# Six operations that wait for transfers keep their program place on their engine

## The chip, the cores and the metric

The kernel runs on one core of a Trainium2 chip. The metric is device time in microseconds (us), the median of three runs. One more execution was recorded by the hardware profiler; its rows are what the text argues from.

## What is computed

One inference step of a small decoder: a pooling layer, then a layer of dilated sliding-window attention, for a prompt of 2048 rows and for 8 single-row samples. Cut to what matters here (the prompt's attention layer):

```
kv = (rmsnorm(h, g_kv) @ w_kv).reshape(B, T, 3, 2, 16, 64)     # keys and values, 3 groups of 16 heads
k  = rope_partial(kv[..., 0, :, :], pos)                       # rotates 16 of the 64 dims of a head
q  = rope_partial((rmsnorm(h, g_b) @ w_in)[q part], pos)
for g, (window, dil) in enumerate(((128, 1), (512, 4), (2048, 16))):
    s = q @ k.T / 8 in blocks of 128, masked to the window;  m = max(s);  p = exp(s - m);  l = sum(p)
    o[g], lse[g] = p @ v / l, m + log(l)
y = sum_g softmax_g(lse) * o[g] * silu(gate);   h = h + y @ w_out;   out = rmsnorm(h, g_final)
```

The kernel also returns the rotated keys and the values of the last rows.

## The kernel before

Products are made to float32 precision from two parts: a value is split into a high part, rounded by a copy (on ACT), and a low part, the difference (on DVE or POOL). A dense product is three matmuls: high by high, low by high, high by low.

After the pooling layer (to about 830 us) and the first half of the rows (to about 1690 us), half 1 works off dense **units** for 8 pairs of heads p, in each for 3 groups g, and in each of these k, q and v: one unit is 48 matmuls of 512 columns on PE into the accumulators `psd` (L241). Beside this dense stream a generator `prompt_attn()` gives the attention, one **step** for each tick of the dense stream: 16 steps for a group, 48 for a pair, 384 in all. A step's scores `pss` (four matmuls, L1211) go through the masked minimum on DVE (L1218), the exponential on ACT (L1224), transposes `ppt` (L1232), their split (`ph` on ACT, L1244; `pl` on DVE, L1248) and the product with the values `ppo` (L1276, L1278). ACT copies half of the product out (`otmp`, L1283) and DVE joins the two halves (`o_add`, L1301).

The operations that the change names stand in these paths:

- A unit's result is copied by ACT into a buffer `raw` (L837), of which three are in use. For k and q, the class `Rope` gathers the rotated rows of two units into `xs` by six DMAs each (`gather`, L782 to L784), multiplies and adds on DVE (`turn`, L790, L791), scatters them back (L794), and some ticks later splits: ACT makes the high part `rh` (L811), it is stored (L812), two ticks later DVE makes the low part in place (L815), and it is stored (L816). The stores of k's output rows (`o_k0` to `o_k2`) read `raw` before that.
- Attention loads k, q and v back (`kt` L1159, `qt` L1161, copied to a second place by POOL, L1163; `vr` L1183, one buffer). `split_v` makes the values' high part on ACT (L1189) and the low part on POOL (L1190).
- After each group, minima and sums are stored and loaded in another layout (`stats_nat`, L1318, L1320, for two of the three groups). `merge` of a pair starts with two minima on DVE (L1329, L1330), and joins the three groups with weights that PE spreads (`pws`, L1359; L1361 on DVE, L1363 on POOL). Joined rows are stored (L1366), and the output phase after the last merge loads them (`cyt`, L1458).

All loads and stores are issued by SP in one queue, in order. `defer(n, f)` runs f n ticks later in program order. The **order on an engine** is not the program's: a scheduler reorders each engine's instructions ahead of time and issues what by its own timing model is ready earliest, so an instruction can stand ahead of ones that were written before it. On the chip each engine then goes through its list in order; an instruction that waits holds all behind it.

Of the kernel before, what the change touches and what calls it, by code (L numbers as in the profile page):

```python
# [12 lines left out]
F32 = mybir.dt.float32  # L13
F32R = mybir.dt.float32r
# [39 lines left out]
def step_kernel(ctx: ExitStack, tc: tile.TileContext, a: dict):  # L54
    nc = tc.nc
    vec, act, pool, pe = nc.vector, nc.scalar, nc.gpsimd, nc.tensor
    load_dma = store_dma = nc.sync.dma_start

    const = ctx.enter_context(tc.tile_pool(name="const", bufs=1))
    dram = ctx.enter_context(tc.tile_pool(name="dram", bufs=1, space=bass.MemoryType.DRAM))  # L60
# [233 lines left out]
    def defer(ticks, fn):  # L294
        deferred.append([ticks, fn])
# [434 lines left out]
    def permd(ap, g):  # L730
        return ap.rearrange("p (r l) -> p r l", r=DIL[g])
# [36 lines left out]
    class Rope:  # L768
# [6 lines left out]
        def gather(self, kind, p, raw):  # L775
            if self.xs is None:
                self.xs = N.bc.tile([P, HALF], F32, name="xs")
            xs, u = self.xs, len(self.units)
            self.units.append((kind, p, raw))
            for b in range(2):  # L780
                x0, r0 = 32 * u + 16 * b, 64 * b
                load_dma(xs[x0:x0 + 16], raw[r0:r0 + 16])  # L782
                load_dma(xs[64 + x0:72 + x0], raw[r0 + 8:r0 + 16])  # L783
                load_dma(xs[72 + x0:80 + x0], raw[r0:r0 + 8])  # L784
            if u == 1:
                defer(3, self.turn)

        def turn(self):
            xs, g = self.xs, self.g
            vec.tensor_tensor(permd(xs, g), permd(xs, g), perm(N.cs2, g), OP.mult)  # L790
            vec.tensor_add(xs[0:64], xs[0:64], xs[64:128])  # L791
            for u, (kind, p, raw) in enumerate(self.units):
                for b in range(2):
                    load_dma(raw[64 * b:64 * b + 16], xs[32 * u + 16 * b:32 * u + 16 * b + 16])  # L794
                defer(3 + 2 * u, lambda kind=kind, p=p, raw=raw: self.split(kind, p, raw))

        def dst(self, kind, p, x):
            v = qkd[kind][self.g][p].rearrange("h d x n -> (h d) x n")[:, x]
# [2 lines left out]
        def split(self, kind, p, raw):  # L801
            g = self.g
            if kind == 1:
                if g == 2:
                    store_dma(a["o_k2"][self.hf, p], raw)
                elif self.hf == 1 and g == 0:
                    store_dma(a["o_k0"][p], raw[:, HALF - P:])
                elif self.hf == 1:
                    store_dma(a["o_k1"][p], permd(raw, g)[:, :, P:])
            rh = N.bw.tile([P, HALF], F32R, name="rh", bufs=1)  # L810
            act.activation(rh, raw, AF.Copy)  # L811
            store_dma(self.dst(kind, p, 0), permd(rh.bitcast(F32), g))  # L812

            def low():
                vec.tensor_sub(raw.bitcast(F32R), raw, rh.bitcast(F32))  # L815
                store_dma(self.dst(kind, p, 1), permd(raw, g))  # L816
                if self.hf == 1:
                    done[p, g] = done.get((p, g), 0) + 1
            defer(2, low)
# [312 lines left out]
    def prompt_attn():  # L1132
# [52 lines left out]
        def split_v(ci):  # L1185
            b0 = first_block(ci)
            vr = V[ci][:, b0:].rearrange("p b (h d) -> p b h d", h=2)
            vt = V[ci] = tl.tile([P, 5, 2, 2, 64], F32R, name="vt")
            act.activation(vt[:, b0:, :, 0], vr, AF.Copy)  # L1189
            pool.tensor_sub(vt[:, b0:, :, 1], vr, vt[:, b0:, :, 0].bitcast(F32))  # L1190

        def prevs(g, c):
# [93 lines left out]
        def o_add(i):  # L1286
            ci, h = i // 4, (i // 2) % 2
            p, g, c = where(ci)
            r0 = 64 * h
            if g == 0 and h == 0:  # L1290
                OT[p, 0, c] = tot.tile([P, 512], F32, name="ot0", bufs=5)
            elif c == 0 and h == 0:
                OT[p, g] = tot.tile([P, SEQ], F32, name=f"ot{g}")
            ot = (OT[p, 0, c] if g == 0 else OT[p, g])[r0:r0 + 64]
            if g == 2:
                act.activation(ot.rearrange("p (l r) -> p r l", r=16)[:, 4 * c:4 * c + 4],
                               PO.pop(i // 2)[0:64].rearrange("p (r l) -> p r l", r=4), AF.Copy)
                return
            po, otmp = PO.pop(i // 2)
            dst = ot if g == 0 else ot.rearrange("p (l r) -> p r l", r=4)[:, c]  # L1300
            vec.tensor_add(dst, po[0:64], otmp)  # L1301

        def stats_nat(p, g):

# [19 lines left out]
        def merge(p):  # L1324


            cst = CST.pop(p)
            mm = tst.tile([P, 2, 16], F32, name="mm")
            vec.tensor_tensor(mm, cst[:, 0, 0:2], cst[:, 1, 0:2], OP.min)  # L1329
            vec.tensor_tensor(mm, mm, cst[:, 2, 0:2], OP.min)  # L1330
            ee = tst.tile([P, 3, 2, 16], F32, name="ee")
            vec.tensor_sub(ee, mm[:, None].to_broadcast([P, 3, 2, 16]), cst[:, :, 0:2])
            act.activation(ee, ee, AF.Exp)
            el = tst.tile([P, 3, 2, 16], F32, name="el")
            vec.tensor_tensor(el, ee, cst[:, :, 2:4], OP.mult)
            vec.tensor_add(mm, el[:, 0], el[:, 1])
            vec.tensor_add(mm, mm, el[:, 2])
            vec.reciprocal(mm, mm)
            vec.tensor_tensor(ee, ee, mm[:, None].to_broadcast([P, 3, 2, 16]), OP.mult)
            yield  # L1340
            ws = tst.tile([P, 6, 2, 16], F32R, name="ws")
            e6 = ee.rearrange("p g h x -> p (g h) x")
            act.activation(ws[:, :, 0], e6, AF.Copy)
            vec.tensor_sub(ws[:, :, 1], e6, ws[:, :, 0].bitcast(F32))
            store_dma(wrow[p].rearrange("r (t x) -> t r x", x=16),
                      ws.bitcast(F32).rearrange("p r i x -> p (r i) x"))
            yield
            yield
            load = lambda e: load_dma(spread[e % 2][0:12], wrow[p][:, 512 * e:512 * e + 512])
            load(0)  # L1350
            load(1)
            for _ in range(4):
                yield
            for e in range(4):
                cs_ = slice(512 * e, 512 * e + 512)
                out = OT[p, 0, e]
                for g in range(3):
                    ps = ps_tile("s", "pws")
                    pe.matmul(ps, sel[:, g], spread[e % 2].bitcast(F32R), start=True, stop=True)  # L1359
                    t_ = OT[p, g][:, cs_] if g else out  # L1360
                    vec.tensor_tensor(t_, ps, t_, OP.mult)  # L1361
                    if g:
                        pool.tensor_add(out, out, t_)  # L1363
                    yield
                d0 = cs_.start + (NB if cs_.start >= HALF else 0)
                defer(2, lambda out=out, d0=d0: store_dma(yd[p][:, d0:d0 + 512], out))  # L1366
                if e < 2:
                    load(e + 2)
# [251 lines left out]
```

## Time and profile before

| what | us |
|---|---|
| median of 3 runs | 3481.15 (3475.03 to 3481.45) |
| the profiled execution | 3495.7 |
| its span | 3493.7 |
| PE busy in the span | 3212.7 |
| half 1 with attention, 1820 to 3200: PE busy of 1380 | 1296.6 |
| the same: DVE, ACT, POOL busy | 837.5, 941.7, 541.8 |

Busy time counts matmuls by a modelled end. The granted clock is the share of TensorE's full 2.4 GHz that the chip gave it in a stretch; 0.5 is 1.2 GHz. A wait in the profile is idle time of an engine just before an instruction, named with what ended it.

### The profile page before, as it was taken

What the parts mean: (1) busy time and instruction counts of PE and PEld (TensorE: products, weight loads), DVE (VectorE), ACT (ScalarE), POOL (GpSimd) and SP (SyncE); (2) the same over time, 40 slices, a digit from 0 to 9 for tenths busy, and PEclk for the clock granted to TensorE, in tenths of its full rate; (3) what the DMA queues carried; (4) which work ended last, traced back from release to release, by engine and by line L of the source; (5) the groups of instructions that cost most, each with busy time, mean ns of one, the idle gap of its engine ahead of it and who ended that gap; (6) DMA issues with size and microseconds to landing.
All of it is one profiled execution on the core that took longest, in us unless ns stands there. A gap on an engine that the chain in (4) does not pass through costs nothing.

```text
span 3493.7 us, 56933 instructions
## 1 busy us (share of the span) xinstructions
PE 3212.7 (92%) x19608; PEld 2821.1 (81%) x19608; DVE 2086.5 (60%) x4061; ACT 1715.9 (49%) x3812; POOL 1516.5 (43%) x954
## 2 busy tenths in 40 slices
PE   8999999899998898987999999899999999999798
PEld 8887778789888887886778788788778878887698
DVE  6745665526766677677346565656565756564445
ACT  3343433324434343343236667675667666778221
POOL 5666765633334354343333343434343434342342
PEclk9999999999999999998999999999999999999899
DMA  4435452424576766767776767676676777775554
GB/s 134 149 123 167 133 165 98 133 91 133 157 196 194 184 196 184 191 203 198 198 219 172 193 183 191 185 172 183 170 202 175 192 182 190 202 193 137 188 154 121
DMA packets 547742, 596.94 MB, mean 171 GB/s; under 512 B 216904, under 2 KB 407752, under 8 KB 547448
## 3 DMA queue, kind: packets, MB, share of 16 engines
q1 hardware_dynamic: 547456, 593.32, 60.7%
q8 instruction: 156, 2.56, 0.3%
q14 instruction: 130, 1.06, 0.1%
HBM read 371.77 MB, written 184.04 MB: 159 GB/s over the span
## 4 chain that ended last, share of the span: by engine, by line
PE 30%; DMA 11%; DVE 6%; SPq 4%; ACT 4%; issue 3%; POOL 1%; DVEq 0%; ACTq 0%; POOLq 0%
PE psd L241 19%; PE pss L1211 3%; PE ppt L1232 3%; DMA statd<-st 1%; PE ppo L1276 1%; DMA xs<-raw 1%; DMA o_k<-raw 1%; PE ppo L1278 1%; ACT pr L1224 1%; DVE xs L791 1%; DMA spb<-pd 1%; PE ppo L1273 1%; DMA raw<-xs 1%; SPq L783 1%; DMA vr<-vd 1%
## 5 line engine op out<-in xcount | busy, mean ns | idle before, releaser
L1163 POOL CAST qt<-qt 64x1024 fp32r<-64x1024 f32 x192 | 209.5, 1091 | 549.4 <-DMA qt<-qd 480.2
L1224 ACT ACTIVATE pr<-pr,st 128x256 f32<-128x256 f32 (+1 forms) x768 | 345.7, 452 | 168.1 <-DVE st L1218 166.3
L1218 DVE CUSTOM_DVE_ANT_0 pr<-pss,mask 128x256 f32<-128x256 f32 (+1 forms) x768 | 248.9, 359 | 154.8 <-PE pss L1211 86.4
L1248 DVE TENSOR_TENSOR pl<-ppt,ph 128x512 fp32r<-128x512 f32 (+2 forms) x384 | 216.9, 569 | 134.1 <-ACT ph L1244 132.0
L168 POOL TENSOR_TENSOR ringl<-wst,ringh 128x1024 fp32r<-128x1024 f32 x96 | 241.3, 2516 | 126.6 <-ACT ringh L163 74.9
L1211 PE MATMUL pss<-kt,qt 128*128 128x256 f32 (+1 forms) x1536 | 268.9, 292 | 27.6 <-DVE st L1218 16.5
L1211 PEld LDWEIGHTS pss<-kt,qt 128*128 128x128 f32 x1536 | 229.0, 199 | 47.2 <-DVE st L1218 18.9
L241 PE MATMUL psd<-hn_2h,ringh 128*128 128x512 f32 x640 | 260.6, 407 | 4.2 <-ACT raw L837 2.4
L241 PE MATMUL psd<-hn_2l,ringh 128*128 128x512 f32 x640 | 259.7, 406 | 5.1 <-DVE hn_2l L644 5.1
L163 ACT ACTIVATE ringh<-wst 128x1024 fp32r<-128x1024 f32 x184 | 193.4, 1052 | 142.2 <-PE psd L241 94.5
L241 PE MATMUL psd<-hn_3h,ringh 128*128 128x512 f32 x640 | 259.6, 406 | 3.0 <-ACT raw L837 1.5
L127 POOL TENSOR_TENSOR wst<-wst,gvec 128x1024 f32<-128x1024 f32 x88 | 178.7, 2033 | 192.1 <-DMA wst<-in_wKV 117.0
L241 PE MATMUL psd<-hn_3l,ringh 128*128 128x512 f32 x640 | 258.8, 404 | 2.2 <-DVE hn_3l L644 2.2
L241 PE MATMUL psd<-hn_2h,ringl 128*128 128x512 f32 x640 | 259.8, 406 | 0.0
L241 PE MATMUL psd<-hn_3h,ringl 128*128 128x512 f32 x640 | 259.3, 405 | 0.0
L1244 ACT ACTIVATE ph<-ppt 128x512 fp32r<-128x512 f32 (+2 forms) x384 | 190.7, 501 | 114.2 <-PE ppt L1232 111.4
L1232 PE MATMUL ppt<-ident,pr 128*128 128x128 f32 x1200 | 211.2, 284 | 22.0 <-DVE pl L1248 10.1
L168 DVE TENSOR_TENSOR ringl<-wst,ringh 128x512 fp32r<-128x512 f32 x176 | 141.6, 841 | 123.3 <-ACT ringh L163 122.9
L1276 PE MATMUL ppo<-ph,vt 128*128 128x128 f32 (+1 forms) x688 | 175.2, 282 | 27.5 <-DVE ot L1301 10.3
L970 PE MATMUL pwx<-t1h,ringh 128*128 128x256 f32 (+1 forms) x576 | 172.1, 299 | 30.3 <-DVE pairl L924 15.8
L1190 POOL TENSOR_TENSOR vt<-vr,vt 128x512 fp32r<-128x512 f32 (+1 forms) x96 | 142.5, 1484 | 127.7 <-ACT vt L1189 107.7
L1232 PEld LDWEIGHTS ppt<-ident,pr 128*128 128x128 f32 x1200 | 145.4, 144 | 49.1 <-issue 11.8
(298 smaller groups left out, 9769.6 us busy)
## 6 DMA issues: line engine op xcount, KB each, us to landing
qt<-qd SPq DMA_DIRECT2D x192, 256.0 KB
wst<-in_wKV SPq DMA_DIRECT2D x72, 512.0 KB
kt<-kd SPq DMA_DIRECT2D x288, 128.0 KB
wst<-in_wA SPq DMA_DIRECT2D x64, 512.0 KB
wst<-in_wQ SPq DMA_DIRECT2D x52, 512.0 KB
kd<-rh SPq DMA_DIRECT2D x48, 512.0 KB
qd<-rh SPq DMA_DIRECT2D x48, 512.0 KB
vd<-vt SPq DMA_DIRECT2D x96, 256.0 KB
```

What stands on the lines that cost most here:

```text
L127: pool.tensor_tensor(st, st, gs[:, :, None].to_broadcast([P, KT, P]), OP.mult)
L163: act.activation(self.w[0], self.st, AF.Copy)
L168: self.eng.tensor_sub(self.w[1][:, k], self.st[:, k], self.w[0][:, k].bitcast(F32))
L241: pe.matmul(ps[:, :n], u[:, k, ws], v[:, k, c0:c1], start=(k, i) == order[0], stop=(k, i) == order[-1])
L1163: pool.tensor_copy(qr[64:128], qr[0:64])
L1211: pe.matmul(ps[:, sl], qt[:, x, qc], kt_[:, kc], start=x == 0, stop=x == 1)
L1218: vec.tensor_tensor_reduce(pr[:, lo:], ps[:, sl], mask[:, lo:], 1.0, BIG, OP.add, OP.min, st[:, 0, h, col:col + 1])
L1224: act.activation(pr[:, lo:], pr[:, lo:], AF.Exp, bias=st[:, 0, h, col:col + 1], scale=-1.0, accum_out=st[:, 1, h, col:col + 1])
L1232: pe.transpose(pt[:, (2 * bb + x) * P:(2 * bb + x + 1) * P], pr[:, x * P:(x + 1) * P], ident)
L1244: act.activation(PB[i][0][:, s], pv[:, s], AF.Copy)
L1248: vec.tensor_sub(PB[i][1][:, s], pv[:, s], PB[i][0][:, s].bitcast(F32))
L1276: pe.matmul(po[:, q0:q1], vt[:, kb + 1, h].rearrange("p x d -> p (x d)"), xh, start=first, stop=False, skip_group_check=True)
```

## The change

`tc.keep_in_program_order(ins)`, called `pin` here, ties an instruction to the one written just before it on the same engine: the scheduler may not put it ahead of that one. It adds no wait on the chip. Pinned are L790, L811, L815, L1189, L1301 and L1329. Two counts of ticks change with it: `turn` is deferred by 4 - hf and the split by 4 - hf + 2u, so that half 1 (hf = 1) keeps 3 and 3 + 2u, and half 0 waits a tick longer. Lines of the changed kernel are two higher from L58 on.

```
@@ -55,6 +55,8 @@
     nc = tc.nc
     vec, act, pool, pe = nc.vector, nc.scalar, nc.gpsimd, nc.tensor
     load_dma = store_dma = nc.sync.dma_start
+
+    pin = tc.keep_in_program_order
 
     const = ctx.enter_context(tc.tile_pool(name="const", bufs=1))
     dram = ctx.enter_context(tc.tile_pool(name="dram", bufs=1, space=bass.MemoryType.DRAM))
@@ -783,16 +785,16 @@
                 load_dma(xs[64 + x0:72 + x0], raw[r0 + 8:r0 + 16])
                 load_dma(xs[72 + x0:80 + x0], raw[r0:r0 + 8])
             if u == 1:
-                defer(3, self.turn)
+                defer(4 - self.hf, self.turn)
 
         def turn(self):
             xs, g = self.xs, self.g
-            vec.tensor_tensor(permd(xs, g), permd(xs, g), perm(N.cs2, g), OP.mult)
+            pin(vec.tensor_tensor(permd(xs, g), permd(xs, g), perm(N.cs2, g), OP.mult))
             vec.tensor_add(xs[0:64], xs[0:64], xs[64:128])
             for u, (kind, p, raw) in enumerate(self.units):
                 for b in range(2):
                     load_dma(raw[64 * b:64 * b + 16], xs[32 * u + 16 * b:32 * u + 16 * b + 16])
-                defer(3 + 2 * u, lambda kind=kind, p=p, raw=raw: self.split(kind, p, raw))
+                defer(4 - self.hf + 2 * u, lambda kind=kind, p=p, raw=raw: self.split(kind, p, raw))
 
         def dst(self, kind, p, x):
             v = qkd[kind][self.g][p].rearrange("h d x n -> (h d) x n")[:, x]
@@ -808,11 +810,11 @@
                 elif self.hf == 1:
                     store_dma(a["o_k1"][p], permd(raw, g)[:, :, P:])
             rh = N.bw.tile([P, HALF], F32R, name="rh", bufs=1)
-            act.activation(rh, raw, AF.Copy)
+            pin(act.activation(rh, raw, AF.Copy))
             store_dma(self.dst(kind, p, 0), permd(rh.bitcast(F32), g))
 
             def low():
-                vec.tensor_sub(raw.bitcast(F32R), raw, rh.bitcast(F32))
+                pin(vec.tensor_sub(raw.bitcast(F32R), raw, rh.bitcast(F32)))
                 store_dma(self.dst(kind, p, 1), permd(raw, g))
                 if self.hf == 1:
                     done[p, g] = done.get((p, g), 0) + 1
@@ -1186,7 +1188,7 @@
             b0 = first_block(ci)
             vr = V[ci][:, b0:].rearrange("p b (h d) -> p b h d", h=2)
             vt = V[ci] = tl.tile([P, 5, 2, 2, 64], F32R, name="vt")
-            act.activation(vt[:, b0:, :, 0], vr, AF.Copy)
+            pin(act.activation(vt[:, b0:, :, 0], vr, AF.Copy))
             pool.tensor_sub(vt[:, b0:, :, 1], vr, vt[:, b0:, :, 0].bitcast(F32))
 
         def prevs(g, c):
@@ -1298,7 +1300,7 @@
                 return
             po, otmp = PO.pop(i // 2)
             dst = ot if g == 0 else ot.rearrange("p (l r) -> p r l", r=4)[:, c]
-            vec.tensor_add(dst, po[0:64], otmp)
+            pin(vec.tensor_add(dst, po[0:64], otmp))
 
         def stats_nat(p, g):
 
@@ -1326,7 +1328,7 @@
 
             cst = CST.pop(p)
             mm = tst.tile([P, 2, 16], F32, name="mm")
-            vec.tensor_tensor(mm, cst[:, 0, 0:2], cst[:, 1, 0:2], OP.min)
+            pin(vec.tensor_tensor(mm, cst[:, 0, 0:2], cst[:, 1, 0:2], OP.min))
             vec.tensor_tensor(mm, mm, cst[:, 2, 0:2], OP.min)
             ee = tst.tile([P, 3, 2, 16], F32, name="ee")
             vec.tensor_sub(ee, mm[:, None].to_broadcast([P, 3, 2, 16]), cst[:, :, 0:2])
```

Every operation and every transfer is the same in both programs, but for two more table loads on ACT (38 against 36). Up to about 1690 us of the trace and from about 3255 us on, all engines have the same order. In between it differs; counted in attention steps, L790, L815 and L811 move back by 16 to 17 steps on average, L1329 by 14, L1189 by 0.4, L1301 by about 0.

DVE at the merge of the sixth pair, before (`pr`, `st` are the scores' minima, `mm` the merge's):

```order
L1248 TENSOR_TENSOR pl<-ppt,ph 128x384
L1301 TENSOR_TENSOR ot_27312<-ppo,otmp 64x512
L1248 TENSOR_TENSOR pl<-ppt,ph 128x512
L1329 TENSOR_TENSOR mm<-cst 128x32
L1218 ISA pr,st_27750<-pss,mask 128x128
L1218 ISA st_27750 128x1
```

and in the changed program:

```order
L1220 ISA pr,st_27750<-pss,mask 128x128
L1220 ISA st_27750 128x1
L1250 TENSOR_TENSOR pl<-ppt,ph 128x2x128
L1324 COPY cst<-st_27750 128x64
L1331 TENSOR_TENSOR mm<-cst 128x32
L1332 TENSOR_TENSOR mm<-mm,cst 128x32
L1334 TENSOR_TENSOR ee<-mm,cst 128x96
```

L1329 (L1331 in the changed program) stood among the minima of the pair's last group; now it stands behind the copy L1322 that ends the pair's statistics, and the second minimum follows at once.

DVE at the low part of one raw buffer, raw_25205, before (with the numbers of the tiles):

```order
L1218 ISA pr_24863,st1_24838<-pss_24839,mask_15543 128x128
L1218 ISA st1_24838 128x1
L1218 ISA pr_24865,st1_24838<-pss_24839,mask_15543 128x256
L1218 ISA st1_24838 128x1
L815 TENSOR_TENSOR raw_25205<-raw_25205,rh_25948 128x1024
L1361 TENSOR_TENSOR ot2_23700<-pws_24867,ot2_23700 128x512
L168 TENSOR_TENSOR ringl_181<-wst_25778,ringh_180 128x512 x2
```

and in the changed program:

```order
L1220 ISA pr_25976,st2_25571<-pss_25956,mask_15543 128x128
L1220 ISA st2_25571 128x1
L1220 ISA pr_25978,st2_25571<-pss_25956,mask_15543 128x128
L1220 ISA st2_25571 128x1
L1250 TENSOR_TENSOR pl_25923<-ppt_25919,ph_25922 128x2x128
L817 TENSOR_TENSOR raw_25205<-raw_25205,rh_25948 128x1024
L1250 TENSOR_TENSOR pl_25967<-ppt_25963,ph_25966 128x2x128
L1220 ISA pr_26029,st2_25571<-pss_26007,mask_15543 128x128
```

The low part stood 140 rows further ahead, just behind the minima of the step that reads pss_24839; now it stands among steps with pss_25956 and pss_26007.

PE from the middle of step 260 on (a row with x4 is four matmuls), before:

```order
L241 MATMUL psd<-hn_3h,ringh 128x512
L1211 MATMUL pss<-kt,qt 128x128 x2
L1211 MATMUL pss<-kt,qt 128x256 x6
L1232 MATMUL ppt<-ident,pr 128x128 x4
L1276 MATMUL ppo<-ph,vt 128x256
L1278 MATMUL ppo<-pl,vt 64x256
L1276 MATMUL ppo<-ph,vt 128x128
L1278 MATMUL ppo<-pl,vt 64x128
L241 MATMUL psd<-hn_3l,ringh 128x512
L241 MATMUL psd<-hn_3h,ringl 128x512
```

and in the changed program:

```order
L243 MATMUL psd<-hn_3h,ringl 128x512
L1213 MATMUL pss<-kt,qt 128x128 x2
L1213 MATMUL pss<-kt,qt 128x256 x2
L1234 MATMUL ppt<-ident,pr 128x128 x2
L1213 MATMUL pss<-kt,qt 128x256 x4
L1278 MATMUL ppo<-ph,vt 128x256
L1280 MATMUL ppo<-pl,vt 64x256
L1278 MATMUL ppo<-ph,vt 128x128
L1280 MATMUL ppo<-pl,vt 64x128
L1234 MATMUL ppt<-ident,pr 128x128 x2
L1213 MATMUL pss<-kt,qt 128x128 x2
```

Before, psd matmuls of the dense units come back after one step. In the changed program the next one stands just ahead of the scores of step 272 (steps are counted from 0). Counted over all 384 steps: runs of at least four steps without a psd matmul are five with 29 steps before, and eight with 69 steps now. Ahead of the first scores of the groups that start at steps 224, 256, 272, 304, 320, 352 and 368, blocks of 55, 31, 65, 47, 82, 54 and 110 psd matmuls stand without attention; before, no block was longer than 26.

## Rows read from the trace of the kernel before

**Rows 1.** The page, busy time of the engines: us, share of the span, instructions.

```profile
PE 3212.7 (92%) x19608; PEld 2821.1 (81%) x19608; DVE 2086.5 (60%) x4061; ACT 1715.9 (49%) x3812; POOL 1516.5 (43%) x954
```

**Rows 2.** Busy time by stage: stretch, its length, busy us (instructions) of PE, PEld, DVE, ACT and POOL, the granted clock of PE, the DMA share, GB/s.

```profile
1690.00:1820.00 130.00, 119.06 (x517) 95.20 (x516) 52.89 (x69) 37.83 (x56) 45.28 (x23) 0.96 0.73 204
1820.00:3200.00 1380.00, 1296.60 (x8044) 1120.37 (x8043) 837.45 (x2364) 941.72 (x2453) 541.79 (x399) 0.96 0.71 186
3200.00:3323.00 123.00, 98.39 (x563) 85.54 (x562) 50.21 (x120) 55.03 (x111) 37.54 (x37) 0.86 0.51 160
```

**Rows 3.** Who waited for whom, 1820 to 3200 us: engine, tile and line <- what ended the wait: us in all, times, longest.

```profile
DVE mm L1329 <- DMA cst<-statd: 43.5, 7, 9.9
ACT vt L1189 <- DMA vr<-vd: 39.7, 14, 7.8
DVE raw L815 <- DMA o_k<-raw: 38.9, 15, 5.5
...
DVE ot L1301 <- DMA yd<-ot: 28.6, 12, 4.0
...
DVE xs L790 <- DMA xs<-raw: 20.5, 13, 3.5
ACT rh L811 <- DMA raw<-xs: 19.5, 15, 3.3
...
ACT rh L811 <- DVE raw L815: 7.4, 6, 2.3
```

**Rows 4.** The timeline of DVE, then of PE, around 2820 us: start, us, operation, and in brackets the idle time ahead of it and what ended it.

```profile
2825.88 0.19 DVE L1329 TENSOR_TENSOR mm<-cst 128x32 f32<-128x32 f32 x1 [9.89 <-DMA cst<-statd]
...
2826.54 0.69 PE L1211 MATMUL pss<-kt,qt 128*128 128x128 f32 x2 [5.62 <-DVE st L1218]
```

**Rows 5.** Busy time ahead of that gap and with it, columns as in Rows 2.

```profile
2812.00:2820.00 8.00, 8.00 (x52) 7.07 (x51) 3.00 (x9) 3.97 (x12) 1.03 (x1) 1.00 0.72 78
2820.00:2830.00 10.00, 4.38 (x18) 3.46 (x17) 3.22 (x12) 4.67 (x13) 1.26 (x1) 0.69 0.45 111
```

**Rows 6.** Busy time in the five stretches without a psd matmul, columns as in Rows 2; then, of L241 alone, the sum over the five; then, of L1211 alone (PE, PEld, clock, DMA), the first and the last of the five, which have 107 matmuls in all.

```profile
2052.00:2068.00 16.00, 11.72 (x54) 9.80 (x53) 11.25 (x27) 10.26 (x26) 7.61 (x5) 0.62 0.87 249
2243.60:2270.50 26.90, 18.60 (x106) 17.45 (x107) 19.10 (x57) 20.56 (x56) 11.55 (x9) 0.75 0.76 224
2458.00:2470.00 12.00, 8.30 (x48) 7.66 (x48) 9.71 (x23) 9.17 (x25) 1.25 (x2) 0.72 0.93 189
2588.90:2604.00 15.10, 8.85 (x44) 7.52 (x43) 11.45 (x27) 8.58 (x20) 5.37 (x6) 0.71 0.76 230
2788.00:2801.00 13.00, 8.61 (x50) 7.51 (x49) 10.31 (x25) 10.19 (x30) 5.28 (x5) 0.74 0.85 259
...
sum 83.00, PE 0.00 PEld 0.05; mean PE 0.00 PEld 0.01
...
2052.00:2068.00 16.00, 4.75 (x19) 3.79 (x17) 0.62 0.87 249
...
2788.00:2801.00 13.00, 4.13 (x20) 3.31 (x19) 0.74 0.85 259
```

**Rows 7.** Who waited in these stretches: the first and the last of the four long waits of PE (3.8, 3.1, 3.8 and 4.0 us).

```profile
PE pvt L861 <- DVE pl L1248: 3.8, 1, 3.8
...
PE ppo L1276 <- ACT rh L811: 4.0, 1, 4.0
```

**Rows 8.** Groups of instructions by line, ACT in 1690 to 3323 us: count | busy us, mean ns of one | idle ahead of them and what ended it.

```profile
L1224 ACT ACTIVATE pr<-pr,st 128x256 f32<-128x256 f32 (+1 forms) x768 | 345.7, 452 | 168.1 <-DVE st L1218 166.3
...
L1244 ACT ACTIVATE ph<-ppt 128x512 fp32r<-128x512 f32 (+2 forms) x384 | 190.7, 501 | 114.2 <-PE ppt L1232 111.4 <-DVE st L1218 0.5
...
L1283 ACT ACTIVATE otmp<-ppo 64x512 f32<-64x512 f32 x128 | 76.3, 596 | 36.2 <-DVE ot L1301 33.4
```

**Rows 9.** Of L837 alone, one of the lines that tell what it waited for: us, times.

```profile
  DMA kd<-raw: 2.3, 1
```

**Rows 10.** The chain that ended last, in order of time (start, us, what): a low or high part stored, a q load. Then the group of POOL's copy of q, and two psd matmuls in PE's timeline.

```profile
2335.70 5.78 DMA kd<-rh
...
1797.06 5.40 DMA qt<-qd
...
L1163 POOL CAST qt<-qt 64x1024 fp32r<-64x1024 f32 x192 | 209.5, 1091 | 549.4 <-DMA qt<-qd 480.2
...
2813.01 0.40 PE L241 MATMUL psd<-hn_3h,ringh 128*128 128x512 f32 x1
2813.24 0.39 PE L241 MATMUL psd<-hn_3l,ringh 128*128 128x512 f32 x1
```

**Rows 11.** The tail: busy time of L241 alone in the last merge; PE's timeline at the first pws of that merge and at the first matmul of the output phase; the group of L1361.

```profile
3227.00:3255.00 28.00, 23.91 (x94) 17.11 (x93) 1.00 0.19 63
...
3230.70 0.74 PE L1359 MATMUL pws<-spread,sel 128*128 128x512 f32 x2 [0.95 <-DMA spread<-wrow]
...
3267.04 0.58 PE L241 MATMUL psd<-cy0h,wbh 128*128 128x288 f32 x1 [12.52 <-DMA cyt<-yd]
...
L1361 DVE TENSOR_TENSOR ot<-pws,ot 128x512 f32<-128x512 f32 x96 | 65.5, 684 | 25.6 <-PE pws L1359 21.7 <-ACT ot L1296 3.5
```

**Rows 12.** Groups of instructions by line, table loads of ACT.

```profile
L1224 ACT ACT_TABLE_LOAD x10 | 12.8, 1283 | 0.2
```

More of the change, by code (lines that the diff above doesn't have):

```diff
@@ L57, in step_kernel @@
     load_dma = store_dma = nc.sync.dma_start
+    pin = tc.keep_in_program_order
     const = ctx.enter_context(tc.tile_pool(name="const", bufs=1))
@@ L785, in gather @@
             if u == 1:
-                defer(3, self.turn)
+                defer(4 - self.hf, self.turn)
         def turn(self):
             xs, g = self.xs, self.g
-            vec.tensor_tensor(permd(xs, g), permd(xs, g), perm(N.cs2, g), OP.mult)
+            pin(vec.tensor_tensor(permd(xs, g), permd(xs, g), perm(N.cs2, g), OP.mult))
             vec.tensor_add(xs[0:64], xs[0:64], xs[64:128])
@@ L794, in turn @@
                     load_dma(raw[64 * b:64 * b + 16], xs[32 * u + 16 * b:32 * u + 16 * b + 16])
-                defer(3 + 2 * u, lambda kind=kind, p=p, raw=raw: self.split(kind, p, raw))
+                defer(4 - self.hf + 2 * u, lambda kind=kind, p=p, raw=raw: self.split(kind, p, raw))
         def dst(self, kind, p, x):
@@ L810, in split @@
             rh = N.bw.tile([P, HALF], F32R, name="rh", bufs=1)
-            act.activation(rh, raw, AF.Copy)
+            pin(act.activation(rh, raw, AF.Copy))
             store_dma(self.dst(kind, p, 0), permd(rh.bitcast(F32), g))
             def low():
-                vec.tensor_sub(raw.bitcast(F32R), raw, rh.bitcast(F32))
+                pin(vec.tensor_sub(raw.bitcast(F32R), raw, rh.bitcast(F32)))
                 store_dma(self.dst(kind, p, 1), permd(raw, g))
@@ L1188, in split_v @@
             vt = V[ci] = tl.tile([P, 5, 2, 2, 64], F32R, name="vt")
-            act.activation(vt[:, b0:, :, 0], vr, AF.Copy)
+            pin(act.activation(vt[:, b0:, :, 0], vr, AF.Copy))
             pool.tensor_sub(vt[:, b0:, :, 1], vr, vt[:, b0:, :, 0].bitcast(F32))
@@ L1300, in o_add @@
             dst = ot if g == 0 else ot.rearrange("p (l r) -> p r l", r=4)[:, c]
-            vec.tensor_add(dst, po[0:64], otmp)
+            pin(vec.tensor_add(dst, po[0:64], otmp))
         def stats_nat(p, g):
@@ L1328, in merge @@
             mm = tst.tile([P, 2, 16], F32, name="mm")
-            vec.tensor_tensor(mm, cst[:, 0, 0:2], cst[:, 1, 0:2], OP.min)
+            pin(vec.tensor_tensor(mm, cst[:, 0, 0:2], cst[:, 1, 0:2], OP.min))
             vec.tensor_tensor(mm, mm, cst[:, 2, 0:2], OP.min)
```

## The prediction

> **What bounds the kernel now.** I read the page first: PE is busy 92% of the span [rows 1], so the time is PE's work plus what PE loses by waiting and by a low clock. Then the busy time by stage [rows 2]. The change moves instructions only between 1690 us and the merge of the last pair at about 3255 us (the order is the same, instruction for instruction, before and after that), so the stage to look at is half 1 with its attention, 1820 to 3200 us. There PE is busy for 1296.6 of 1380 us at a mean granted clock of 0.96: PE's work at the full clock is about 1296.6 x 0.96 = 1245 us, and the loss is 135 us, 83 us of it idle and 52 us clock. No other engine comes near (ACT 942, DVE 837, DMA share 0.71). What can be won here is at most these 135 us, and what can be lost has no such bound.
>
> Third, who waited for whom in that stage [rows 3]. These of its rows belong to the change: on DVE the merge's first minimum L1329 (43.5 us), the low part L815 (38.9), the rotation L790 (20.5); on ACT the high part L811 (19.5, and 7.4 for L815); then the values' high part L1189 (39.7) and the joining L1301 (28.6). Each is an instruction that stands at the head of an in-order engine while its transfer flies, with attention's own operations behind it. One case shows the whole mechanism [rows 4]: L1329 holds DVE for 9.89 us, L1218 stands behind it, and PE, whose next scores wait for a buffer that L1218 frees, has a gap of 5.62 us. The granted clock was 1.00 in the 8 us before; over the 10 us with the gap it was 0.69, partly at 1.2 instead of 2.4 GHz [rows 5]. So a wait costs its gap and some clock behind it.
>
> Fourth, where dense matmuls (psd of the units) are missing beside attention. Five stretches of 83 us in all have no psd matmul, and there PE is busy only 56.1 us, at clocks of 0.62 to 0.75 [rows 6]. Busy time by clock gives 39.9 us of work, so 43 us are lost: a third of the stage's loss in 6% of its time. The scores' matmuls count 107 in them, four to a step, so 27 steps: 1.49 us of work and 1.6 us of loss for each.
>
> **The change part by part.** Nothing is computed otherwise. By the order, measured in attention steps, L790, L815 and L811 move back by 16 to 17 on average, L1329 by 14. L1329 then stands right behind L1322, 14 steps (of 1380/384 = 3.6 us, an estimate: about 50 us) later than before; L790 stands 4 to 17 steps behind its gather where it was about 1, and the six DMAs of the gather have 2 to 5 us to land. So I take these waits as gone. L1301 and L1189 move by less than half a step on average: their waits stay, pins or not. Moved are 43.5 + 38.9 + 20.5 + 19.5 + 7.4 = 130 us of wait, not moved 39.7 + 28.6 = 68 [rows 3], a share of 0.655.
>
> Term 1, the waits outside the psd-free stretches: the loss there is 135 - 43 = 92 us. Taken in proportion to the waits, 0.655 x 92 = 60 us go and 32 stay. This is an estimate; its ends are 92 (all PE loss follows these waits) and about 30 (what is freed meets the next wait in half of the cases).
>
> Term 2, the psd-free stretches. The pins tie the release of a raw buffer (L815, then its store L816) to attention's progress, and the dense stream, which in before ran some 75 to 130 matmuls ahead of attention, can no longer do so. By the order, before has five runs of four or more steps without a psd matmul, 29 steps; after has eight, 69 steps. The price of one step decides the sum. As measured it is 1.6 us, but 14.7 of the 26.9 us that PE idled in these stretches are four gaps that stand right behind a wait of L815 or L811 [rows 7], which go. 12.2 us of idle stay, and of the 16.3 us of clock I keep half: 20.4 us over 27 steps, 0.8 us a step. Its lower end is the pace of ACT, which has the most to do in a step: (345.7 + 190.7 + 76.3)/384 = 1.6 us [rows 8] against PE's 1.49, 0.1 us a step. The upper end is 1.6, if the pinned waits were not what made these stretches slow. With 0.8 the stretches lose 69 x 0.8 = 55 us where they lost 43.
>
> The Trainium skill, page "Perfetto Trace Analysis", section Optimization Strategy, speaks against the change here: where a kernel has regimes that are limited by different engines, it advises to interleave them, and the new order interleaves less. By that rule the step keeps the price that the stretches have now, 1.6 us; the rival below has the time. The rows of the five stretches agree with it.
>
> Term 3, raw buffers. After the change L815 comes on average 4.7 steps ahead of the first write (L837) of the same buffer's next user, where it was 13.7; in 16 of 42 cases it is at most 2. L837 then can wait for the store on ACT, with attention's exponentials behind it. Before shows one such wait, of 2.3 us [rows 9]. At 0 to 1.5 us of PE time for each of the 16 that is 0 to 24; I take 8, since a part is already in term 2.
>
> Term 4, starts of groups. From step 224 on, attention has caught up with the dense stream at seven group starts: on PE 31 to 110 psd matmuls stand in one block ahead of the group's first scores, while SP's queue has only some five DMAs, or none, between the last store of the group's q and its first load. The chain store, load, cast is 5.78 + 5.40 + 1.09 = 12.3 us [rows 10]. A psd matmul takes 0.233 us, start to start [rows 10], so the blocks cover 7.2 us (31), 10.9 (47) and 12.6 us or more (54 to 110): uncovered are 5 and 1.4, together 6 us. The ends are 0 and 7 x 12.3 = 86.
>
> Term 5, the tail. In before, 23.9 us of psd matmuls run between 3227 and 3255 us beside the last merge [rows 11]; in after they are done earlier and the 12 pws stand together. From 3227 us before takes 40.0 us to the first matmul of the output phase (3267.04). After needs 3.7 us to the first pws (3230.70), 12 x 0.684 = 8.2 for L1361, about 1 for the last and the 12.5 us that the first output matmul waits for its load: 25.4, and 23.9 us of psd earlier, +9 us. The ends are -3 (its loads issued during the merge) and +15.
>
> The rest costs nothing that I can find: two table loads more on ACT, 1.28 us each [rows 12], beside PE work on an engine with a third of its time free (if not hidden, 2.6 us). In half 0 the pins and the shifted ticks change no instruction's place.
>
> **Sum.** Stage loss 135 becomes 32 + 55 + 8 + 6 = 101, so -34; the tail adds 9: -25 us. The profiled execution took 3495.7 us, which makes 3470.7; the median of the runs lies 14.5 us under the profiled one, and carries the same change: 3481.15 - 25 = 3456 us.
>
> **Rivals.** (a) Slower: the psd-free steps keep the price of today. 69 x 1.6 = 110 instead of 55 us: the sum is +30 us, 3511. For it: each of the five stretches of before has a low clock, and a clock that is low makes PE itself the slow link there (2243.6 to 2270.5: 18.6 us busy at 0.75). Against it: the four gaps behind pinned waits. It decides from 25/69 us above my value, at about 1.16 us a step.
>
> The Trainium skill, page "TensorE: Matmul & The Clock Gate", section Why this matters for your kernels, warns of idle gaps between bursts of matmuls because the clock falls back to half. The trace agrees where PE had its 5.62 us gap; whether the clock holds in a long attention-only run without such gaps no row here shows.
>
> (b) Slower: group starts uncovered. If the last stores are later than the order makes them look (L816 waits for L815, which is now behind attention steps), all seven chains stand open: +80 us on my sum, 3536. It decides when stores are issued after the dense block begins to run out.
>
> (c) The gain is larger: the stretches run at ACT's pace, 0.1 us a step, 7 us in all: -73, 3408.
>
> (d) No net change: price near 1.16, or what goes at L1329 and L815 returns at L1301, L1189 and L837: about 3481. That the pins do nothing is excluded for four of the six lines by the order; for L1301 and L1189 it is what I expect.
>
> **How the numbers follow.** About 7 us (0.2%) is what a measurement of this kernel can tell from no change. Forecast 0.51, (c) 0.11: faster 0.62. (d) 0.16: same. (a) 0.16, (b) 0.06: slower 0.22. The range must reach (c) and most of (a): 3408 to 3505 leaves out (b), the far end of (a) and what lies beyond (c), in all about 0.18.
>
> **What would show it.** L1329, L790, L815 and L811 should nearly vanish from the list of waits, with L1189 and L1301 at 40 and 30 us or more. PE's busy time times clock in 1820 to 3200 us should stay near 1245 us. The psd-free stretches should be longer, some 69 steps, and their loss by step reads off term 2 directly: 0.8 for me, 1.6 for (a), 0.1 for (c). L837 shows term 3, PE's gaps ahead of pss at seven group starts term 4, the stretch between the last L1322 and the first output matmul term 5. I am wrong if the waits stay where they are, or if the clock in attention-only runs is as low without gaps as with them.

## The result, and the profile after

The changed kernel takes 3526.33 us (3521.99 to 3539.61, 4 runs) beside 3481.3 us of before: 1.0136 of it, 95% interval 1.0120 to 1.0152. It is slower, by about 47 us, and outside the range. The profiled execution of after has a span of 3523.2 us, that of before 3493.7; so the two traces differ by 29.5 us, less than the medians (45): the profiled execution of before is 14 us above its median, that of after close to its own. The accounts below are of these two executions.

Half 1 with attention first, the stretch of [rows 2], from the busy time by stage (columns as there):

```profile
1820.00:3200.00 1380.00, 1286.74 (x7916) 1109.33 (x7915) 830.36 (x2319) 921.82 (x2396) 538.79 (x390) 0.96 0.69 182
```

PE is busy for 10 us less than before at the same clock, and does 128 matmuls less in the same time. To see where the time goes, I cut the work from 1690 us to the end into three pieces, for every kernel in the same way: up to the last scores (the last pss), from there to the first matmul of the output phase, and the rest. The loss of a piece is its length less PE's busy time by the granted clock, summed over slices of 5 us. Of the first piece the stretches without psd matmuls are taken by themselves (between two psd matmuls with at least 14 pss between them).

| us | before | changed |
|---|---|---|
| loss up to the last pss | 138.7 | 153.5 |
| of it in stretches without psd | 46.9 (34 steps) | 69.8 (77 steps) |
| of it outside them | 91.7 | 83.8 |
| loss from the last pss to the output phase | 13.7 | 27.6 |
| output phase | 226.6 | 223.3 |

23 us come from the stretches and 14 from the last merge; the waits outside give back 8 and the output phase 3. These are 25.5 us. Both pages count the same 19608 matmuls (that of before in [rows 1], this that of the changed kernel):

```profile
PE 3219.5 (91%) x19608; PEld 2819.0 (80%) x19608; DVE 2084.1 (59%) x4061; ACT 1719.5 (49%) x3814; POOL 1521.1 (43%) x954
```

Up to 1690 us the order of the two is the same; but the 9400th matmul starts at 1702.9 us before and at 1697.6 in the changed kernel, so from there on the changed execution is 35 us longer. Some 9 us of these the pieces do not explain, and that stays open.

Who waited, 1820 to 3200 us, columns as in [rows 3] (lines are two higher):

```profile
ACT vt L1191 <- DMA vr<-vd: 70.1, 20, 11.9
...
DVE ot L1303 <- DMA yd<-ot: 42.4, 19, 5.9
...
ACT raw L839 <- DMA kd<-raw: 22.1, 9, 7.0
...
ACT rh L813 <- DMA raw<-xs: 20.2, 11, 3.6
...
DVE ot L1303 <- ACT otmp L1285: 19.6, 14, 12.4
...
DVE raw L817 <- DMA o_k<-raw: 12.8, 5, 7.1
...
PE psd L243 <- ACT raw L839: 11.2, 7, 3.8
...
DVE raw L817 <- DMA kd<-rh: 7.2, 1, 7.2
DVE raw L817 <- issue: 6.2, 1, 6.2
```

The merge's minimum (43.5 us before) and the rotation (20.5) have no row any more. The low part's wait for the output rows fell from 38.9 to 12.8, with 13.4 us of two waits at the same line that before did not have. The high part still waits for its transfer as it did (19.5 before). And three waits for transfers grew: the values' high part from 39.7 to 70.1, the joining from 28.6 to 42.4, and L839 (L837 of before), which hardly waited for a store before [rows 9], now waits 22.1 us for raw buffers to be stored, with PE's psd matmuls behind it. What went is 43.5 + 20.5 + 26.1 + 7.4 = 97.5 us, what came is 30.4 + 13.8 + 22.1 + 13.4 = 80.

This list leaves out other waits at the same lines: the joining's wait for `otmp`, above all, fell from 34.7 to 19.6 us. All idle time ahead of the six pinned lines and L837, whatever ended it, was 276 us before and is 233 now. So 43 us of wait did go on DVE and ACT, and PE's loss outside the stretches fell by 8.

The stretches without psd matmuls, as in [rows 6], with the sum of L243 alone and the first and the last row of L1213 alone (308 pss in all, 77 steps):

```profile
1837.60:1864.60 27.00, 21.95 (x161) 20.40 (x160) 24.06 (x65) 23.61 (x61) 11.28 (x9) 0.87 0.78 216
2045.00:2071.40 26.40, 20.18 (x141) 17.47 (x139) 24.62 (x64) 22.74 (x62) 11.92 (x9) 0.94 0.80 225
2372.70:2387.50 14.80, 10.98 (x61) 9.57 (x60) 11.23 (x29) 9.95 (x29) 5.08 (x4) 0.77 0.80 186
2563.40:2596.10 32.70, 23.78 (x167) 20.40 (x165) 28.29 (x75) 27.05 (x76) 14.31 (x10) 0.95 0.78 211
2766.10:2797.30 31.20, 22.94 (x164) 20.62 (x163) 26.96 (x71) 27.19 (x76) 12.28 (x9) 0.89 0.77 191
2849.30:2860.20 10.90, 8.71 (x70) 8.03 (x69) 6.44 (x26) 10.83 (x31) 2.32 (x2) 0.84 0.83 254
2964.20:2993.80 29.60, 21.34 (x133) 19.02 (x131) 25.48 (x55) 23.16 (x61) 8.93 (x5) 0.81 0.69 156
3036.10:3062.10 26.00, 20.10 (x151) 18.56 (x150) 17.17 (x65) 22.91 (x66) 9.81 (x8) 0.79 0.83 238
...
sum 198.60, PE 3.24 PEld 0.58; mean PE 0.41 PEld 0.07
...
1837.60:1864.60 27.00, 8.15 (x44) 6.66 (x44) 0.87 0.78 216
...
3036.10:3062.10 26.00, 8.51 (x44) 7.83 (x44) 0.79 0.83 238
```

There are eight stretches instead of five, at clocks of 0.77 to 0.95 instead of 0.62 to 0.75. A step costs 69.8/77 = 0.91 us there; it cost 1.4 before by the same cut. ACT and DVE are busy for 84% and 83% of these stretches.

The tail: DVE's copy that ends the last statistics, PE's first pws of the last merge and its first output matmul, then the busy time of that stretch:

```profile
3262.27 0.20 DVE L1324 COPY cst<-st 128x64 f32<-128x64 f32 x1 [1.60 <-ACT pr L1226]
...
3272.10 0.73 PE L1361 MATMUL pws<-spread,sel 128*128 128x512 f32 x2 [3.38 <-DMA spread<-wrow]
...
3299.84 0.58 PE L243 MATMUL psd<-cy0h,wbh 128*128 128x288 f32 x1 [16.99 <-DMA cgt<-sgd]
...
3267.10:3299.80 32.70, 8.99 (x25) 4.04 (x23) 13.37 (x24) 8.12 (x13) 14.20 (x13) 0.59 0.71 206
```

PE is busy for 9 of 32.7 us, at a clock of 0.59; before, 23.9 us of psd matmuls stood in the merge [rows 11].

A start of a group, at step 224 (2600 us): SP's store of q's low part, its load of the group's q, POOL's copy of it and PE's first scores:

```profile
2597.68 0.39 SPq L818 DMA_DIRECT2D qd<-raw  x1
...
2608.78 1.83 SPq L1163 DMA_DIRECT2D qt<-qd  x3
...
2617.22 1.03 POOL L1165 CAST qt<-qt 64x1024 fp32r<-64x1024 f32 x1 [12.37 <-DMA qt<-qd]
...
2618.31 1.97 PE L1213 MATMUL pss<-kt,qt 128*128 128x128 f32 x8 [3.45 <-POOL qt L1165]
```

From the store's issue to the first scores 20.6 us go by, and not the 12.3 of the forecast: SP issues the load 11.1 us behind the store, and in between the rest of a gather, another gather, and attention's loads of k and v. The block of 55 psd matmuls covers all but 3.45 us of it. Slice by slice the seven starts lose some 12 to 14 us together, by where a slice is cut from the stretches beside it.

### The profile page after: what moved, and what is told of

Same layout as the page of the kernel before. It is cut to its first block, busy times and chain, and to the rows that moved or that the text cites. A ratio compares the mean times of both kernels' runs of the same rounds, so it can differ in the third digit from the quotient of the medians.

```text
span 3523.2 us, 56875 instructions
## 1 busy us (share of the span) xinstructions
PE 3219.5 (91%) x19608; PEld 2819.0 (80%) x19608; DVE 2084.1 (59%) x4061; ACT 1719.5 (49%) x3814; POOL 1521.1 (43%) x954
## 4 chain that ended last, share of the span: by engine, by line
PE 33%; DMA 9%; DVE 6%; SPq 4%; ACT 3%; issue 3%; POOL 1%; DVEq 0%; ACTq 0%; POOLq 0%
PE psd L243 21%; PE pss L1213 3%; PE ppt L1234 2%; PE pwx L972 1%; DMA wst<-in_wKV 1%; DMA cyt<-yd 1%; PE ppo L1278 1%; DVE pr L1220 1%; PE ppo L1275 1%; PE ppo L1280 1%; ACT pr L1226 1%; DVE pl L1250 1%; DMA statd<-st 1%; DMA kd<-raw 1%; DVE xs L793 1%
## 5 line engine op out<-in xcount | busy, mean ns | idle before, releaser
L1165 POOL CAST qt<-qt 64x1024 fp32r<-64x1024 f32 x192 | 218.3, 1138 | 493.3 <-DMA qt<-qd 395.5
L1213 PE MATMUL pss<-kt,qt 128*128 128x256 f32 (+1 forms) x1536 | 263.5, 294 | 24.6 <-issue 9.6
L243 PE MATMUL psd<-hn_2h,ringh 128*128 128x512 f32 x640 | 263.5, 412 | 22.1 <-ACT raw L839 20.2
L243 PE MATMUL psd<-hn_2l,ringh 128*128 128x512 f32 x640 | 261.4, 408 | 5.1 <-DVE hn_2l L646 5.1
L243 PE MATMUL psd<-hn_3h,ringh 128*128 128x512 f32 x640 | 259.7, 406 | 6.5 <-ACT raw L839 2.7
L243 PE MATMUL psd<-hn_2h,ringl 128*128 128x512 f32 x640 | 261.6, 409 | 0.0
L243 PE MATMUL psd<-hn_3l,ringh 128*128 128x512 f32 x640 | 258.6, 404 | 2.0 <-DVE hn_3l L646 2.0
L1213 PEld LDWEIGHTS pss<-kt,qt 128*128 128x128 f32 x1536 | 225.7, 199 | 42.1 <-issue 13.5
L243 PE MATMUL psd<-hn_3h,ringl 128*128 128x512 f32 x640 | 258.9, 405 | 0.0
L170 DVE TENSOR_TENSOR ringl<-wst,ringh 128x512 fp32r<-128x512 f32 x176 | 149.3, 886 | 174.9 <-ACT ringh L165 174.3
```

The costliest lines, as they stand in the source:

```text
L170: self.eng.tensor_sub(self.w[1][:, k], self.st[:, k], self.w[0][:, k].bitcast(F32))
L243: pe.matmul(ps[:, :n], u[:, k, ws], v[:, k, c0:c1], start=(k, i) == order[0], stop=(k, i) == order[-1])
L1165: pool.tensor_copy(qr[64:128], qr[0:64])
L1213: pe.matmul(ps[:, sl], qt[:, x, qc], kt_[:, kc], start=x == 0, stop=x == 1)
```

## The experiments

Theory A after the result: what the pins on rotation and parts (L790, L811, L815) do is to take the dense stream's lead over attention away; psd matmuls then stop beside attention, attention meets its own loads, and nothing is left to cover the last merge. Rivals: the other three pins do it (B); one piece does all of it; the pins cost by themselves. All diffs are against the changed kernel. Ratios are to before, measured again beside each run (3482 to 3488 us). "Free steps" are the steps in runs without a psd matmul, by the order.

**e1, e2: half of the pins each.** e1 takes away the pins on rotation and parts, e2 the other three:

```
e1:  pin(...) -> ...   at L792, L813, L817
e2:  pin(...) -> ...   at L1191, L1303, L1331
```

> Only the values' high part, the joining and the merge's minimum keep their place; rotation and both parts of the rotated rows float as before. By its order it has 29 steps in runs without a psd matmul (before 29, changed kernel 69) and 109 psd matmuls left behind the last scores (before 124, changed kernel 29). Theory A (the pins on rotation and parts hold the raw buffers, so psd matmuls stop beside attention, and none is left to cover the last merge): faster than before, since only the 43.5 us of waits at L1329 go: 3462 to 3476. Rival B (the pins on L1189, L1301 and L1329 are what costs, through their own engines): 3500 or more.

> Only rotation and the two parts of the rotated rows are pinned. By its order 77 steps in runs without a psd matmul and 34 psd matmuls behind the last scores. Theory A: the whole loss of the changed kernel or more, 3525 to 3545. Rival B: 3480 or less.

e1: 0.9974 of before (0.9957 to 0.9991), faster by 9 us (12 by the medians). e2: 1.0124 (1.0090 to 1.0158), the whole loss. Both times, 3473.11 and 3529.27, lie in theory A's ranges, and B falls. By pieces, with 46.9 us in the stretches and 91.7 outside them before, e2 loses 94.3 and 70.2, e1 38.1 and 69.2. The pair shows which pins cost, not yet by what. e1's stage (busy time, columns as above):

```profile
1820.00:3200.00 1380.00, 1310.92 (x8223) 1130.10 (x8222) 845.56 (x2411) 964.15 (x2506) 544.49 (x405) 0.98 0.70 187
```

**e3, e4, e6: one pin of the three.**

```
e3:  only L792 keeps pin(...)
e4:  only L817 keeps pin(...)
e6:  only L813 keeps pin(...)
```

> Only the rotation L790 is pinned. By its order 66 steps in runs without a psd matmul, but 99 psd matmuls stand behind the last scores, so the last merge is covered. Theory A1 (the steps without a psd matmul cost about as much as the uncovered last merge): 3495 to 3510. Rival A2 (the uncovered last merge is nearly all of it): 3472 to 3484.

> Only the low part L815 is pinned. By its order 30 steps in runs without a psd matmul and 125 psd matmuls behind the last scores: neither cost of theory A is there, and the 38.9 us that DVE waited at L815 should go. If a wait on DVE that goes is time won at PE's share of it (83 of 198 us): 16 us less, 3465. Rival D (what goes there returns at the next wait): 3477 to 3485.

> Only the high part L811 is pinned. By its order 49 steps in runs without a psd matmul (20 more than before), and no psd matmul behind the last scores. At 0.75 to 0.95 us for a step (from the run with the rotation alone pinned) 15 to 19 us, and 14 for the uncovered last merge: 29 to 33 us, 3510 to 3517. If an uncovered merge costs nothing by itself: 3498 to 3503. If the rotation alone does the harm: 3480 to 3487.

e3: 1.0086 (1.0056 to 1.0117), 28 us slower; its 3512.26 is 2 us above A1's range. Its stretches lose 76.8 us (before 46.9), its tail only 17.8: the steps cost without the uncovered merge. Outside the stretches it loses 76.0, 16 less than before. e6: 1.0111 (1.0093 to 1.0128), 40 us slower and above the expected range. Its stretches lose as little as before (46.1), its tail 31.8, but 112.5 us are lost outside the stretches (before 91.7); there the low part waits 46.8 us for the high part, against 8.4 before:

```profile
DVE raw L817 <- ACT rh L813: 46.8, 26, 5.6
```

So the account by free steps and tail alone is too narrow. The three don't add up (28 + 40 + 8 us against 45 together, by the medians): the rotation alone and the high part alone each cost most of it, the low part alone little.

e4: 1.0025 (1.0008 to 1.0041), D rather than the gain, though 3492.57 is 8 us above D's range. Its waits, columns as above:

```profile
ACT raw L839 <- DMA qd<-raw: 20.5, 8, 5.3
...
PE psd L243 <- ACT raw L839: 12.1, 9, 3.5
...
DVE raw L817 <- DMA o_k<-raw: 4.3, 3, 3.8
```

The low part's own wait went from 38.9 to 4.3 us, and the raw buffer, stored later, is waited for by L839 instead, with PE behind. Here the exchange is seen with one pin alone, at the next user of the same buffer; the order around it differs in many places too.

**e5, e12: the other pins.**

```
e5:   only L1331 keeps pin(...)
e12:  only L1191 and L1303 keep pin(...)
```

> Only the merge's first minimum L1329 is pinned. 34 steps in runs without a psd matmul, 156 psd matmuls behind the last scores. If the 43.5 us of waits at L1329 are what the run with the three pins L1189, L1301 and L1329 won (12 us): 3468 to 3477. If that gain came from the other two pins: 3480 or more.

> Only L1189 and L1301 are pinned. 28 steps in runs without a psd matmul, 157 psd matmuls behind the last scores. The minimum alone gained nothing and the three together 9 us: if L1189 and L1301 gain it, 3474 to 3482; if it takes all three, 3484 to 3492.

e5: 1.0016 (1.0001 to 1.0032), no gain, though the 43.5 us of waits at L1331 are gone from its trace. Other lines have grown there (39.7, 20.5 and 19.5 us before); that they grew because the minimum moved is not shown:

```profile
ACT vt L1191 <- DMA vr<-vd: 50.1, 21, 6.3
...
DVE xs L792 <- DMA xs<-raw: 31.0, 14, 4.6
ACT rh L813 <- DMA raw<-xs: 30.0, 17, 5.4
```

e12: 1.0051 (1.0031 to 1.0072), slower than both expectations. Alone neither part gains what the three gain together; why e12 loses was not found. Its order has neither more free steps nor a shorter cover, and its loss outside the stretches is 104.3 us.

**e7, e8: a fourth raw buffer.** It has no room without a control:

```
e7:  kt bufs=3 -> 2, raws bufs=3 -> 2 (same tag), pr bufs=6 -> 5
e8:  as e7, and
-        if N.bw2 is not None and N.nraw % 3 == 0:
-            return N.bw2.tile([P, HALF], F32, name="raw3")
+        if N.bw2 is not None and N.nraw % 4 > 1:
+            return N.bw2.tile([P, HALF], F32, name="raw3", bufs=2)
```

> The control for the next run: the changed kernel with two kt buffers for three and five pr buffers for six, which makes room. By its order 82 steps in runs without a psd matmul, none of the dense matmuls behind the last scores: 10 to 25 us slower than the changed kernel, 3537 to 3552.

> The control with a fourth raw buffer. By its order 54 steps in runs without a psd matmul, 28 fewer than the control, and no psd matmul behind the last scores either. If raw buffers held by the pinned operations are what stops the psd matmuls, and each such step costs 0.9 us: 25 us faster than the control, 3512 to 3527. If the steps cost nothing by themselves: within 5 us of the control.

e7: 3579.14 us, 1.0274 of before (27 us above its expected range); e8: 3563.45 us, 16 us faster than e7 on the same chip, between the two expectations (25 and under 5); its time is 36 us above its expected range, because the control already was. The loss in the stretches fell from 111.9 to 43.5 us, but outside them it rose from 80.7 to 133.4. The raw buffers do stop the psd matmuls; where those run instead, most of the gain is lost again, by what was not found.

**e9, e10, e11, e13, e14: the lead back, without touching the pins.** Attention's first step is traced some ticks later, so that the dense stream is ahead in the program itself:

```
         nq = nv = ns = t = 0
+        for _ in range(16):          # e10, e11: 8   e14: 24
+            yield
         while t < n_steps + 7 or extra:
e9, e10, e14: all six pins   e11: the pins of e1   e13: 16 ticks, no pin
```

> The changed kernel, all six pins kept, with attention's first step traced 16 ticks later, so that the dense stream is 16 ticks further ahead in program order. By its order 31 steps in runs without a psd matmul (changed kernel 69, before 29), one block of more than 30 psd matmuls after step 100 (changed kernel 7), 63 psd matmuls behind the last scores. If the changed kernel's loss comes from the lead that the dense stream lost to the pins: the loss goes and the waits at L1329 and L790 stay away: 3465 to 3485. If the pins cost by themselves (raw buffers held until the low part's place): 3510 or more.

> The same with 8 ticks. 35 steps in runs without a psd matmul, three blocks (76, 42 and 98) late, 39 psd matmuls behind the last scores. Lead: 3485 to 3505, between the changed kernel and the run with 16. Pins by themselves: 3510 or more.

> The run with pins on L1189, L1301 and L1329 alone, with attention traced 8 ticks later. 25 steps in runs without a psd matmul, 93 psd matmuls behind the last scores. There the dense stream can float ahead without help, so the lead in the program should give little: 3468 to 3482, the same as without it within 6 us.

> No pins at all, attention traced 16 ticks later. 23 steps in runs without a psd matmul (before 29), no block over 31, but only 18 psd matmuls behind the last scores (before 124). If the uncovered last merge costs by itself what the traces show (14 us more loss behind the last scores): 3492 to 3502. If it costs nothing: 3475 to 3485.

> All six pins, attention traced 24 ticks later. 37 steps in runs without a psd matmul, one block of 35, 44 psd matmuls behind the last scores. If what the run with 16 ticks still lost (13 us) is the last merge and the waits that the pins don't take away: no better, 3492 to 3506. If it is lead: 3475 to 3488.

| kernel | of before | 95% interval | loss in stretches | outside | tail |
|---|---|---|---|---|---|
| changed | 1.0136 | 1.0120 to 1.0152 | 69.8 | 83.8 | 27.6 |
| e10, pins, 8 | 1.0120 | 1.0092 to 1.0148 | 60.8 | 100.6 | 23.5 |
| e9, pins, 16 | 1.0039 | 1.0021 to 1.0057 | 39.1 | 91.9 | 22.0 |
| e14, pins, 24 | 1.0063 | 1.0046 to 1.0080 | 50.4 | 85.9 | 22.0 |
| e13, no pins, 16 | 1.0021 | 1.0007 to 1.0034 | 29.7 | 88.3 | 33.7 |
| e11, pins of e1, 8 | 1.0055 | 1.0039 to 1.0072 | 42.5 | 107.7 | 16.8 |

The pieces are of one execution each: that of e14 is the fastest of its four and 14 us below its median, that of before is as much above its own.

e9 takes back two thirds of the loss with every pin in place; its time, 3495.88, is above the expected 3485 and below 3510. With 8 ticks (e10) hardly anything comes back: 3527.06 lies where the pins would cost by themselves (3510 or more), not where the lead would put it. Its order has as few free steps as e9 (35 and 31), but three late blocks, of 42 to 98 psd matmuls; that these are the reason is not shown. More than 16 (e14) gives nothing more: 3507.89, 2 us above the first reading's range. e13 beside e9 has the same lead with and without pins, 1.0021 against 1.0039; the intervals overlap, so with this lead no cost of the pins is clear of the noise. In e13 the joining and the values' high part wait 30.3 and 23.9 us (e9: 61.8 and 55.4), while the minimum and the rotation, unpinned, wait again (43.5 and 20.5 before). In e13:

```profile
DVE mm L1331 <- DMA cst<-statd: 34.3, 7, 9.2
DVE ot L1303 <- DMA yd<-ot: 30.3, 14, 4.4
DVE xs L792 <- DMA xs<-raw: 28.3, 13, 5.7
...
ACT vt L1191 <- DMA vr<-vd: 23.9, 12, 7.8
```

In e9:

```profile
DVE ot L1303 <- DMA yd<-ot: 61.8, 19, 6.2
...
ACT vt L1191 <- DMA vr<-vd: 55.4, 20, 5.8
```

e13 also prices the cover: its stage loses 118.0 us, 21 less than before, and its tail 33.7, 20 more. Its time, 3490.81, lies between its two expectations, close to the one in which the merge costs. e11 was expected at e1's time and took 0.8% more; its rotation and its high part wait 45 us each (e1: 29 and 25). That where floating operations end up decided more there than the lead is a guess.

So the lead accounts for a part: 16 ticks take back 1.0%, which is more than the 0.5% by which orders without a known fault (e11, e12) differ from before. That the pins cost nothing by themselves is not shown, since e10 has a lead too and lost nearly all of the 1.36%.

## Why the prediction was wrong

- **Term 1, the waits outside the stretches, is the step that failed most.** The prediction: "So I take these waits as gone", 130 us of wait, 60 us of loss. Measured: 97.5 us of wait for transfers went, 80 came; with all waits counted the seven lines lost 43 us. The loss outside the stretches fell by 8 us, where terms 1, 3 and 4 together made it 46. There were three errors. L811 moves back by 16 steps, but so does the transfer it waits for, since the whole chain of a rotation moves: it waits 20.2 us for it with the rotation pinned too, while in e6, where it is pinned alone, no row for this transfer is left. Second, "their waits stay, pins or not" was true of the place of L1301 and L1189, not of their transfers: these waits grew by 44 us. Third, PE's loss does not follow these waits in proportion: 43 us less of wait gave 8, what the group starts cost included. e4 shows an exchange with one pin alone, and e5 a wait that went without a gain.
- **Term 2: mechanism right, size off.** The psd-free steps came as the order said (69 counted, 77 in the trace). The price is 0.91 us, where 0.8 was forecast; the 1.6 of rival (a) did not come. But the price is no constant: by the same cut it is 1.4 in before, 0.65 in e4 (47 steps, 30.4 us) and 1.27 in e10 (48 steps, 60.8 us), so that 0.91 lies near 0.8 is in part luck. The stretches lost 47 us before and lose 70 now: 23 us instead of 12. e3 shows the steps at work with the last merge still covered; e6 and e8 show that the same time can be lost outside them as well.
- **Term 3 and term 4** were forecast at 8 and 6 us. L839's 11.2 us of PE time in the stage (and 22.1 on ACT) and some 12 to 14 us at the group starts are above that, and both lie in the loss outside the stretches. Rival (b) asked for seven open chains; the blocks covered most of them.
- **Term 5: near, in part by luck.** +9 was forecast; the traces show +14 in the merge and -3 in the output phase. From the first pws to the first output matmul 21.7 us were forecast and 27.7 went by: that matmul waited 16.99 us, and for another load (`cgt`) than in before.
- **The sum.** Stage 135 to 101 was forecast; the trace has 139 to 154. None of the rivals was the case as told: (a), the nearest with 3511, had too high a price, (b) too much open, (d) too little returned. The prediction names the lead of 75 to 130 matmuls, but prices it only as free steps and group starts. In e9, with 16 ticks of lead traced back in, the same pins cost 0.4%; that the lead kept waits from reaching PE is the reading that this supports, and e10 does not fit it.
- The sentence of the page "Perfetto Trace Analysis", section Optimization Strategy, that regimes with different limits should be interleaved (the Trainium skill) pointed the right way: with 69 steps and seven blocks apart the kernel lost. Its reading as a price of 1.6 us a step did not hold. On the clock, what was open is now seen: in the attention-only stretches of the changed kernel it was 0.77 to 0.95, and in each of them it fell to half for a time, though the longest gap of PE in any was 2.1 us. By its sign of being wrong (a clock as low without gaps as with them) the prediction stands in part: the four stretches of before with a gap of 3.1 to 4.0 us had 0.71 to 0.75, but the fifth, at 0.62, had none above 1.84.

What stays open: why three pins that alone give +0.2% (e5) and +0.5% (e12) give -0.3% together (e1), why eight ticks make e1 slower by 0.8%, and why they do not help the six pins where sixteen do. Each order differs in hundreds of places, and no single wait was found that carries these differences. The best version found is e1, 3473.11 us.

## What to carry to other kernels

An instruction that is moved back along with its whole chain can wait as long as before (L811: 19.5 and 20.2 us); look at its distance to the transfer that it waits for, not at how far it moves, and look for the wait at whoever uses the buffer next (e4). Before an operation is tied to its program place, ask what lead its stream has by floating: where two streams cover each other, the pins took that lead away here, and writing 16 ticks of it into the program order (e9) took back two thirds of the loss. Count in the new order how many steps run without the other stream, and what is left to cover the end.

## What the runs showed that I had not expected

The same program in other orders, with no work added, takes 3473 to 3529 us (e1 to e6, without the runs that change buffers). And PE's gaps do not tell the clock of an attention-only stretch. The stretch at 2563 to 2596 us, with no gap above 1.19 us, ran at 0.95, that at 2964 to 2994, with one of 2.14, at 0.81; in before, four with a gap of 3.1 to 4.0 us had 0.71 to 0.75, and the one at 2052 to 2068, whose longest was 1.84, had 0.62. The longest gaps of the first two, from PE's timeline, and PE's longest wait in the last:

```profile
2591.94 0.39 PE L1278 MATMUL ppo<-ph,vt 128*128 128x256 f32 x1 [1.19 <-POOL vt L1192]
...
2973.33 0.87 PE L1234 MATMUL ppt<-ident,pr 128*128 128x128 f32 x3 [2.14 <-DVE pl L1250]
...
PE ppt L1232 <- DVE s L1313: 1.8, 1, 1.8
```
